# Half-steps of a decoder trunk: evictions scheduled ahead of weights' parts, three leads, a later combine, six last outputs of chunk 1

## The chip, the core and the metric

One NeuronCore of one Trainium2 chip runs the whole program; the other cores are idle. The metric is the device time of one execution in microseconds (us), lower is better. The kernel before takes 2192.76 us, the median of three runs (2188.43 to 2197.22).

## The reference

A trunk of two layers works on 512 prompt tokens and 8 sample tokens, 520 columns in all, of 1024 features. Each layer is a half-step feed-forward, a mixer (differential attention beside gated linear attention in layer 0, a matrix memory in layer 1), and another half-step feed-forward:

```python
def swiglu(x, w_gate, w_up, w_down):
    return (jax.nn.silu(x @ w_gate) * (x @ w_up)) @ w_down

def macaron_half(x, g, w_gate, w_up, w_down):
    return x + (0.5 * swiglu(rmsnorm(x, g), w_gate, w_up, w_down)).astype(x.dtype)
```

`w_gate` and `w_up` are 1024 x 2816, `w_down` is 2816 x 1024, all float32. The change touches the four half-steps and nothing else. In the order of the program the stages are: half-step 1, mixer 1, half-step 2, half-step 3, mixer 2, half-step 4. Half-steps 2 and 3 follow each other directly.

## The kernel before, in words

**Layout.** Activations lie transposed: features on 128 partitions in 8 tiles (`KT`), tokens along the columns in two chunks, chunk 0 of 256 columns and chunk 1 of 264 (`CH`). A float32 product is made of three matmuls of a narrower type: every operand is split into a rounded high part and the rest (`split`, lines 110 to 112: a cast on ScalarE, L111, then a subtraction on VectorE, L112), and `dense` (L106 to L108) issues high x high, high x low and low x high. So each weight tile costs a cast and a subtraction besides its transfer.

**A half-step** works through 22 tiles of 128 hidden features, in groups of 6, 6, 6 and 4 (`GROUPS`). The first four tiles (`LEAD = 4`) are *leads*: gate and up products in the plain way, `early`, 8 weight tiles for the gate, 8 for the up product, two chunks. While TensorE works on them, VectorE and ScalarE norm the input and form the sums and differences that the rest needs (`begin` and `then`, generators whose parts are called by `step()` between products). All later gate tiles are *units* of a seven-product scheme in the manner of Strassen and Winograd (`Unit.product`): gate and up features are one 2 x 2 side, the two halves of the features and the two chunks the other, and seven products (p1, q5, q6, p2, p3, p7, p4) of 4 weight tiles each do the work of eight. Three banks A, B and E take them: p1, q6, p7 and p4 accumulate in A one after the other, p2 in B on a copy of p1, q5 and p3 in E. So each product but the first has to wait until the one before it in its bank has been read out (evicted): `Gate.out`, with `c5` for q5 (L515), `f.h(1)` for q6 (L517), a Silu for p2 (L519), additions for p3 and p7 (L521 to L525) and a multiply for p4 (L528). p4 of a unit is issued behind p1 and q5 of the next one.

**Weights of a unit** (`weights`, L418 to L439): a transfer of g (two blocks, tag `graw`, two buffers), one of u, one of a block that is written twice into s (tag `raw`, three buffers in the pool `wraw`), all on SP's queue, and an accumulating transfer on POOL's queue (L429) that adds two further blocks into s. Then `parts` splits g, u and s, two additions (L432) turn g into further sums, and it is split again. The split halves go to the pool `whl` with five buffers. All of this is in `tc.high_priority(AHF)` with AHF = 200.

**The order of the work** is made when the kernel is built: a scheduler simulates the engines and always takes the instruction with the best priority among those that it thinks are ready; priority is the place in the program, and `tc.high_priority(n)` treats instructions as though they stood n places earlier. [...]

**Pairs.** Two gate tiles form a `Pair`, whose four results lie in one tile `h` (L452 to L456). `open` takes it: tag `stg` (one buffer) for the first pair, `graw` for the second while leads run, `stg` for the others, and a small memset on POOL. When both tiles are done, `combine` (L465 to L474) forms three sums and differences on VectorE and splits all seven parts into `hidden`, which is what the *down* units (`Down`, the second matrix, again seven products, evicted into x by L552) read. In the kernel before, both pairs of the leads are combined inside the first unit, behind its q5 (L600 to L605).

**The end of a half-step** (L636 to L651): the last group's hidden features are multiplied in the plain way, 8 outputs x 2 chunks, each 4 weight tiles x 3 matmuls. The first `KT - lag` outputs are done in both chunks; the last `lag` ones first in chunk 0 and then in chunk 1, so that the norm of chunk 0 for the next stage (`norm_lead` before another half-step, `norm_ahead` before a mixer: statistics on TensorE, a chain of short VectorE operations in `rsqrt`, then `norm_apply`, L173, with a multiply and a split per feature tile) can run beside chunk 1's outputs. `lag` is 4, and 0 in the last half-step. The split weights of these last outputs are held until chunk 1 has used them.

Of the kernel before, what the change touches and what calls it, by code (L numbers as in the profile page):

```python
# [7 lines left out]
F32 = mybir.dt.float32  # L8
# [7 lines left out]
P = 128  # L16
# [7 lines left out]
LEAD = 4  # L24
CH = ((0, 256), (256, 264))
UNIT = 8
# [11 lines left out]
AHM, AHF, AHE = 1, 200, 100  # L38
WHL = 5
# [22 lines left out]
class Net:  # L62
# [12 lines left out]
    def fetch(self, u):  # L75
        if self.raw[0] != u:
            raw = self.wraw.tile([P, UNIT * P], F32, tag="raw", name="raw")
            self.wq.dma_start(out=raw, in_=self.t["w"][u])
            self.raw = (u, raw)
# [185 lines left out]
    def half_step(self, pos, first, last, xp, hp, pa):  # L265
# [10 lines left out]
        H = KT // 2  # L276
        n0, n1 = CH[0][1], CH[1][1]
# [140 lines left out]
        def weights(f):  # L418

            B = f.nk * P  # L420
            w = self.t["w"]
            g = hp.tile([P, 4 * n1], F32, tag="graw", name="graw", bufs=2)[:, :2 * B]
            self.wq.dma_start(out=g, in_=w[f.u0, :, :2 * B])
            u = hp.tile([P, H * P], F32, tag="u2", name="u2")[:, :B]
            self.wq.dma_start(out=u, in_=w[f.u0 + 1, :, :B])
            s = self.wraw.tile([P, 2 * H * P], F32, tag="raw", name="raw")[:, :2 * B]
            s2 = s.rearrange("p (u c) -> p u c", u=2)
            self.wq.dma_start(out=s2, in_=w[f.u0 + 1, :, None, B:2 * B].to_broadcast([P, 2, B]))
            nc.gpsimd.dma_start(out=s2, in_=w[f.u0:f.u0 + 2, :, :B].rearrange("u p c -> p u c"), accum_op=ALU.add)  # L429

            def add(x, y):
                nc.vector.tensor_tensor(out=x, in0=x, in1=y, op=ALU.add)  # L432
            with tc.high_priority(AHF):
                f.w = parts(g, B, 2, ("g1", "g2"))
                f.w |= parts(u, B, 1, ("u2",))
                f.w |= parts(s, B, 2, ("s3", "s1"))
                add(g[:, :B], s[:, B:])
                add(g[:, B:], g[:, :B])
                f.w |= parts(g, B, 2, ("s2", "s4"))  # L439
# [7 lines left out]
        class Pair:  # L447

            def __init__(self, i, plain):
                self.i, self.plain, self.h = i, plain, None  # L450

            def open(self, tag="stg"):  # L452
                if self.h is None:
                    self.h = hp.tile([P, 4 * n1], F32, tag=tag, name="h",
                                     bufs=2 if tag == "graw" else None).rearrange("p (s t) -> p s t", s=4)
                    nc.gpsimd.memset(self.h[:, 0:3:2, n0:], 0.0)  # L456
# [8 lines left out]
            def combine(self):  # L465
                x11, x22, x21, x12 = [self.h[:, i] for i in range(4)]
# [8 lines left out]
        self_split = self.split  # L475
# [5 lines left out]
        class Unit:  # L481

            def product(f, kind):
# [11 lines left out]
                f.out(kind, ps[:, :n])  # L495
                step()

        class Gate(Unit):
# [11 lines left out]
            def out(f, kind, ps):  # L510
# [16 lines left out]
                elif kind == "p4":  # L527
                    nc.vector.tensor_tensor(out=f.h(0), in0=ps, in1=f.h(0), op=ALU.mult)  # L528
                    f.done(0)
                    if f.odd and not f.pair.plain:  # L530
                        f.pair.combine()
# [24 lines left out]
        for gi, nf in enumerate(GROUPS):  # L556
            plain = gi == len(GROUPS) - 1
            pairs = [Pair(i, plain) for i in range(nf // 2)]
# [12 lines left out]
        leads, seq = seq[:LEAD], seq[LEAD:]  # L571
# [7 lines left out]
        while i < LEAD:  # L579
# [4 lines left out]
            for f in fs:  # L584
                f.pair.open("stg" if i < 2 else "graw")
# [10 lines left out]
        for f in seq:  # L596
# [3 lines left out]
            if before is None:  # L600
# [3 lines left out]
                for p in (leads[0].pair, leads[2].pair):  # L604
                    p.combine()  # L605
# [6 lines left out]
            for kind in ("q6", "p2", "p3", "p7"):  # L612
                f.product(kind)
            before = f
# [22 lines left out]
        lag = 0 if last else 4  # L637
# [1296 lines left out]
```

## Time and profile before

| | us |
|---|---|
| median of three runs | 2192.76 |
| lowest, highest | 2188.43, 2197.22 |
| the profiled execution | 2194.01 |
| its span in the trace | 2192.2 |
| TensorE matmul busy | 2130.5 |
| VectorE busy | 1629.2 |
| ScalarE busy | 1108.1 |

The span runs from the first to the last instruction of the program. PE is TensorE's matmuls, PEld its weight loads, DVE VectorE, ACT ScalarE, POOL GpSimd, SP the queue that issues most transfers. A busy matmul is no sure sign of full speed, since matmuls overlap: the number started in a stretch (x415 in 50 us) says more. [...] In a row of the waits view or in brackets, "<- ACT h L655" names what ended the wait: the instruction at line 655 on ScalarE that writes tile h. Tile names are those of the program: A, B, E the banks of the units, g and u those of the leads, y those of the last outputs, pj the mixers' first tiles, c the tile of q5.

### The profile page before, as it was taken

The page shows a single profiled execution, that of the slowest core. Times are in us where ns is not written, and L with a number is a line of the kernel's source. Part 1 is how long each engine was busy: PE and PEld are TensorE (multiplying, and loading weights), DVE is VectorE, ACT ScalarE, POOL GpSimd, SP SyncE. Part 2 cuts the span into 40 slices and gives each one's busy share as a digit, 9 for nine tenths or more (in the row PEclk, how much of TensorE's full clock was granted, in tenths as well). Part 3 has the DMA queues.
Part 4 walks back from the last instruction along what each step waited for, and adds up shares of the span by engine and source line. Part 5 has one row for each costly group of instructions (what it writes and reads, how often), then busy time and mean ns, then how long its engine had stood idle before and what let it go on. Part 6 is the DMA issues. An engine that isn't in the chain of part 4 may idle for free.

```text
span 2192.2 us, 46399 instructions
## 1 busy us (share of the span) xinstructions
PE 2130.5 (97%) x17908; PEld 2001.1 (91%) x17908; DVE 1629.2 (74%) x3409; ACT 1108.1 (51%) x2080; POOL 194.6 (9%) x276
## 2 busy tenths in 40 slices
PE   8999999999999999999999999999999999999999
PEld 8899999776776799999999999998989899999999
DVE  8888887434486587888877888877745588788884
ACT  6555555334523354556554565654555456455653
POOL 1011101000000001111100111100000000111110
PEclk9999999999999999999999999999999999999999
DMA  7487764478787745867733677653554564676872
GB/s 214 118 207 169 180 169 144 155 261 264 233 264 249 240 143 128 209 159 191 186 126 84 167 179 193 161 147 94 149 158 147 167 195 152 139 204 166 191 182 73
DMA packets 175763, 381.29 MB, mean 174 GB/s; under 512 B 16353, under 2 KB 51730, under 8 KB 175414
## 3 DMA queue, kind: packets, MB, share of 16 engines
q1 hardware_dynamic: 129600, 283.23, 39.6%
q0 software_dynamic: 40176, 82.05, 20.9%
q10 hardware_dynamic: 5766, 13.05, 1.6%
q8 instruction: 140, 2.29, 0.4%
q14 instruction: 81, 0.66, 0.1%
HBM read 361.15 MB, written 17.11 MB: 173 GB/s over the span
## 4 chain that ended last, share of the span: by engine, by line
PE 74%; DVE 13%; DMA 9%; ACT 3%; issue 2%; SPq 0%; ACTq 0%; DVEq 0%; POOLq 0%
PE A L106 9%; PE A L108 8%; PE A L107 8%; PE E L106 4%; PE E L107 4%; PE E L108 4%; DVE wlo L112 4%; PE pj L106 4%; PE pj L108 3%; PE pj L107 3%; PE y L106 2%; DMA raw<-w 2%; PE y L107 2%; PE y L108 2%; PE B L108 2%; PE B L107 2%
## 5 line engine op out<-in xcount | busy, mean ns | idle before, releaser
L112 DVE TENSOR_TENSOR wlo<-raw,whi 128x512 fp32r<-128x512 f32 (+2 forms) x344 | 311.9, 910 | 106.1 <-ACT whi L111 101.6
L111 ACT CAST whi<-raw 128x512 fp32r<-128x512 f32 (+2 forms) x344 | 273.2, 799 | 153.8 <-PE pj L107 76.6
L112 DVE TENSOR_TENSOR wlo<-graw,whi 128x1024 fp32r<-128x1024 f32 (+1 forms) x240 | 266.4, 1115 | 113.3 <-ACT whi L111 112.2
L111 ACT CAST whi<-graw 128x1024 fp32r<-128x1024 f32 (+1 forms) x240 | 231.2, 965 | 154.4 <-PE B L107 90.0
L106 PE MATMUL pj<-xh,whi 128*128 128x264 f32 (+1 forms) x896 | 258.8, 291 | 4.3 <-ACT kT L655 1.5
L106 PE MATMUL A<-xb,whi 128*128 128x264 f32 (+1 forms) x864 | 250.8, 290 | 8.2 <-DVE c L524 4.7
L108 PE MATMUL pj<-xh,wlo 128*128 128x264 f32 (+1 forms) x896 | 254.3, 285 | 1.5 <-DVE wlo L112 1.5
L107 PE MATMUL pj<-xl,whi 128*128 128x264 f32 (+1 forms) x896 | 255.0, 285 | 0.8 <-DVE xl L112 0.7
L107 PE MATMUL A<-xb,whi 128*128 128x264 f32 (+1 forms) x864 | 244.7, 283 | 0.6 <-DVE xb L112 0.6
L108 PE MATMUL A<-xb,wlo 128*128 128x264 f32 (+1 forms) x864 | 245.0, 284 | 0.0
L429 POOL DMA_DIRECT2D raw<-w x120 | 142.1, 1184 | 1141.3 <-DMA raw<-w 402.7
L106 PEld LDWEIGHTS pj<-xh,whi 128*128 128x128 f32 x896 | 169.1, 189 | 20.5 <-issue 9.5
L106 PEld LDWEIGHTS A<-xb,whi 128*128 128x128 f32 x864 | 163.4, 189 | 13.4 <-DVE c L524 5.9
L107 PEld LDWEIGHTS pj<-xl,whi 128*128 128x128 f32 x896 | 169.6, 189 | 5.1 <-DVE xl L112 2.5
L108 PEld LDWEIGHTS pj<-xh,wlo 128*128 128x128 f32 x896 | 169.6, 189 | 4.5 <-issue 2.7
L106 PE MATMUL A<-hh,whi 128*128 128x264 f32 (+1 forms) x576 | 165.5, 287 | 2.0
L106 PE MATMUL E<-xh,whi 128*128 128x264 f32 x576 | 163.6, 284 | 3.9 <-ACT c L655 3.9
L107 PEld LDWEIGHTS A<-xb,whi 128*128 128x128 f32 x864 | 163.1, 189 | 0.8 <-DVE xb L112 0.8
L107 PE MATMUL E<-xl,whi 128*128 128x264 f32 x576 | 163.4, 284 | 0.0
L108 PEld LDWEIGHTS A<-xb,wlo 128*128 128x128 f32 x864 | 163.3, 189 | 0.0
L108 PE MATMUL E<-xh,wlo 128*128 128x264 f32 x576 | 163.2, 283 | 0.0
L107 PE MATMUL A<-hl,whi 128*128 128x264 f32 (+1 forms) x576 | 162.7, 282 | 0.0
(491 smaller groups left out, 6266.9 us busy)
## 6 DMA issues: line engine op xcount, KB each, us to landing
raw<-w SPq DMA_DIRECT2D x168, 512.0 KB, 4.2
raw<-w POOLq DMA_DIRECT2D x112, 512.0 KB, 6.9
graw<-w SPq DMA_DIRECT2D x72, 512.0 KB, 4.2
kt<-ckt SPq DMA_DIRECT2D x128, 256.0 KB, 4.4
vtile<-cv SPq DMA_DIRECT2D x128, 256.0 KB, 4.0
u<-w SPq DMA_DIRECT2D x72, 256.0 KB, 3.7
raw<-w SPq DMA_DIRECT2D x48, 384.0 KB, 3.7
raw<-w POOLq DMA_DIRECT2D x48, 384.0 KB, 5.6
```

The costliest lines, as they stand in the source:

```text
L106: nc.tensor.matmul(ps, lhsT=wh, rhs=xh, start=(ends[0] and i == ks[0]), stop=False, skip_group_check=open_)
L107: nc.tensor.matmul(ps, lhsT=wh, rhs=xl, start=False, stop=False, skip_group_check=open_)
L108: nc.tensor.matmul(ps, lhsT=wl, rhs=xh, start=False, stop=(ends[1] and i == ks[-1]), skip_group_check=open_)
L111: self.nc.scalar.copy(out=hi, in_=src)
L112: self.nc.vector.tensor_tensor(out=lo, in0=src, in1=hi, op=ALU.subtract)
L429: nc.gpsimd.dma_start(out=s2, in_=w[f.u0:f.u0 + 2, :, :B].rearrange("u p c -> p u c"), accum_op=ALU.add)
```

## The change

Five things, all in the half-steps. (1) The number of leads is 4 in the program's first half-step and 3 in the others; the tile that was a lead becomes a unit. (2) `f.out`, the eviction of a product, runs at `high_priority(AHO)` with AHO = 300, ahead of the weights' parts at 200; what followed p4 there, the combine, moves into a new `after` behind it. (3) `combine` runs at `high_priority(AHC)`, AHC = 100; the leads' first pair is combined behind all products of the first unit instead of inside it, the second pair inside it only where there are four leads (with three it is half a lead and half a unit, and is combined as every other). (4) The tiles of pairs: with four leads the first group's pairs take `stg`, `graw` and `raw`, with three `stg`, `raw`, `stg`; all others `stg`. For that, `raw` tiles grow from 1024 to 1056 columns. (5) `lag` is 6 instead of 4, still 0 in the last half-step.

```diff
@@ -21,7 +21,8 @@
 T = SEQ + NS
 DFF = 2816
 GROUPS = (6, 6, 6, 4)
-LEAD = 4
+LEAD = 4, 3
+
 CH = ((0, 256), (256, 264))
 UNIT = 8
 EPS = 1e-6
@@ -36,6 +37,7 @@
 REST = 4
 
 AHM, AHF, AHE = 1, 200, 100
+AHO, AHC = 300, 100
 WHL = 5
 SLOPE = [2.0 ** (-2 * (h + 1)) for h in range(4)]
 
@@ -74,7 +76,7 @@
 
     def fetch(self, u):
         if self.raw[0] != u:
-            raw = self.wraw.tile([P, UNIT * P], F32, tag="raw", name="raw")
+            raw = self.wraw.tile([P, 4 * CH[1][1]], F32, tag="raw", name="raw")[:, :UNIT * P]
             self.wq.dma_start(out=raw, in_=self.t["w"][u])
             self.raw = (u, raw)
 
@@ -274,6 +276,7 @@
 
         nc, tc = self.nc, self.tc
         H = KT // 2
+        lead = LEAD[not first]
         n0, n1 = CH[0][1], CH[1][1]
         xh, xl, x = self.xh, self.xl, self.x
         xb = [xp.tile([P, 3, H, n1], F32R, tag=f"xb{i}", name="xb") for i in range(2)]
@@ -423,7 +426,7 @@
             self.wq.dma_start(out=g, in_=w[f.u0, :, :2 * B])
             u = hp.tile([P, H * P], F32, tag="u2", name="u2")[:, :B]
             self.wq.dma_start(out=u, in_=w[f.u0 + 1, :, :B])
-            s = self.wraw.tile([P, 2 * H * P], F32, tag="raw", name="raw")[:, :2 * B]
+            s = self.wraw.tile([P, 4 * n1], F32, tag="raw", name="raw")[:, :2 * B]
             s2 = s.rearrange("p (u c) -> p u c", u=2)
             self.wq.dma_start(out=s2, in_=w[f.u0 + 1, :, None, B:2 * B].to_broadcast([P, 2, B]))
             nc.gpsimd.dma_start(out=s2, in_=w[f.u0:f.u0 + 2, :, :B].rearrange("u p c -> p u c"), accum_op=ALU.add)
@@ -446,13 +449,14 @@
 
         class Pair:
 
-            def __init__(self, i, plain):
-                self.i, self.plain, self.h = i, plain, None
-
-            def open(self, tag="stg"):
+            def __init__(self, i, plain, tag):
+                self.i, self.plain, self.h, self.tag = i, plain, None, tag
+
+            def open(self):
                 if self.h is None:
-                    self.h = hp.tile([P, 4 * n1], F32, tag=tag, name="h",
-                                     bufs=2 if tag == "graw" else None).rearrange("p (s t) -> p s t", s=4)
+                    pool = self_wraw if self.tag == "raw" else hp
+                    self.h = pool.tile([P, 4 * n1], F32, tag=self.tag, name="h",
+                                       bufs=2 if self.tag == "graw" else None).rearrange("p (s t) -> p s t", s=4)
                     nc.gpsimd.memset(self.h[:, 0:3:2, n0:], 0.0)
 
             def slot(self, odd, c):
@@ -463,6 +467,10 @@
                 self_split(hidden[0][:, self.i, j:j + b - a], hidden[1][:, self.i, j:j + b - a], self.h[:, a:b])
 
             def combine(self):
+                with tc.high_priority(AHC):
+                    self.combined()
+
+            def combined(self):
                 x11, x22, x21, x12 = [self.h[:, i] for i in range(4)]
                 cm = hp.tile([P, 4 * n1], F32, tag="cmb", name="cmb").rearrange("p (s t) -> p s t", s=4)
                 nc.vector.tensor_tensor(out=cm[:, 0:2], in0=self.h[:, 0:2], op=ALU.subtract,
@@ -472,7 +480,7 @@
                 nc.vector.scalar_tensor_tensor(cm[:, 3], cm[:, 2], -1.0, x21, ALU.mult, ALU.subtract)
                 for a in (0, 2):
                     self_split(hidden[0][:, self.i, 3 + a:5 + a], hidden[1][:, self.i, 3 + a:5 + a], cm[:, a:a + 2])
-        self_split = self.split
+        self_split, self_wraw = self.split, self.wraw
         hidden = []
         WHERE = {"p1": ("g1", "x11"), "p2": ("g2", "x21"), "q5": ("s1", "a"), "q6": ("s2", "b"), "p7": ("s3", "c"),
                  "p3": ("s4", "x22"), "p4": ("u2", "d")}
@@ -492,8 +500,13 @@
                            open_=True)
                 if kind == "p1":
                     self.evict(f.B[:, :n0], ps[:, :n0])
-                f.out(kind, ps[:, :n])
+                with tc.high_priority(AHO):
+                    f.out(kind, ps[:, :n])
+                f.after(kind)
                 step()
+
+            def after(f, kind):
+                pass
 
         class Gate(Unit):
             nk = H
@@ -527,8 +540,10 @@
                 elif kind == "p4":
                     nc.vector.tensor_tensor(out=f.h(0), in0=ps, in1=f.h(0), op=ALU.mult)
                     f.done(0)
-                    if f.odd and not f.pair.plain:
-                        f.pair.combine()
+
+            def after(f, kind):
+                if kind == "p4" and f.odd and not f.pair.plain:
+                    f.pair.combine()
 
             def done(f, c):
                 if f.pair.plain and not f.late:
@@ -555,7 +570,8 @@
         seq, gates = [], []
         for gi, nf in enumerate(GROUPS):
             plain = gi == len(GROUPS) - 1
-            pairs = [Pair(i, plain) for i in range(nf // 2)]
+            tags = ["stg"] * 3 if gi else ["stg", "graw", "raw"] if lead == 4 else ["stg", "raw", "stg"]
+            pairs = [Pair(i, plain, tags[i]) for i in range(nf // 2)]
             fs = [Gate(u0 + 2 * j, pairs[j // 2], j % 2) for j in range(nf)]
             gates += fs
             u0 += 2 * nf
@@ -568,7 +584,7 @@
             if not plain:
                 downs = [Down(u0 + 2 * d, d, nf // 2) for d in range(H)]
                 u0 += 2 * H
-        leads, seq = seq[:LEAD], seq[LEAD:]
+        leads, seq = seq[:lead], seq[lead:]
         self.seek(pos)
         if first:
             self.fetch(pos // UNIT)
@@ -576,13 +592,13 @@
             raw(0, range(KT))
         steps.append(begin())
         i = 0
-        while i < LEAD:
+        while i < lead:
             fs = leads[i:i + (2 if i == 0 else 1)]
             ws = [self.weights(2 * KT) for _ in fs]
             if first and i == 0:
                 self.x_load(KT, 2 * KT)
             for f in fs:
-                f.pair.open("stg" if i < 2 else "graw")
+                f.pair.open()
             if i == 0 and not first:
                 step()
             for c in range(2):
@@ -601,8 +617,8 @@
                 while steps:
                     step()
                 hidden += [hp.tile([P, max(GROUPS) // 2, 7, n1], F32R, tag=n, name=n) for n in ("hh", "hl")]
-                for p in (leads[0].pair, leads[2].pair):
-                    p.combine()
+                if lead == 4:
+                    leads[2].pair.combine()
             else:
                 before.product("p4")
                 if isinstance(before, Down) and before is downs[-1]:
@@ -611,6 +627,8 @@
                     p.parts(3, 4, 3)
             for kind in ("q6", "p2", "p3", "p7"):
                 f.product(kind)
+            if before is None:
+                leads[0].pair.combine()
             before = f
         before.product("p4")
         nf = GROUPS[-1]
@@ -634,7 +652,7 @@
             else:
                 self.sq_add(c, d)
         self.gi = self.nxt
-        lag = 0 if last else 4
+        lag = 0 if last else 6
         for d in range(KT - lag):
             w = self.weights(nf)
             down(d, 0, w)
```

## Rows read from the trace of the kernel before

**Rows 1.** The page, part 1: busy time, share of the span, instructions of each engine.

```profile
PE 2130.5 (97%) x17908; PEld 2001.1 (91%) x17908; DVE 1629.2 (74%) x3409; ACT 1108.1 (51%) x2080; POOL 194.6 (9%) x276
```

**Rows 2.** Windows view, full stretches: stretch, us, engines' busy (count), PEclk, DMA, GB/s.

```profile
950.00:1000.00 50.00, 49.98 (x415) 49.67 (x414) 41.41 (x72) 25.88 (x40) 6.05 (x6) 1.00 0.71 181
813.00:842.00 29.00, 29.00 (x243) 29.00 (x243) 17.85 (x23) 12.65 (x19) 4.76 (x4) 1.00 0.68 148
```

**Rows 3.** Timeline, first half-step: start, us, engine, line, names [idle before <- releaser].

```profile
72.86 1.04 ACT L111 CAST whi<-graw 128x1024 fp32r<-128x1024 f32 x1 [2.42 <-DMA graw<-w]
...
75.63 0.11 POOL L456 MEMSET h<- 128x16 f32 x1 [9.15 <-DVE cmb L472]
...
76.52 0.59 PE L106 MATMUL A<-xb,whi 128*128 128x264 f32 x1 [3.55 <-ACT h L655]
```

**Rows 4.** Windows view, first half-step, behind that wait.

```profile
76.40:79.80 3.40, 3.28 (x15) 3.28 (x16) 3.40 (x6) 1.35 (x5) 0.00 (x0) 0.50 0.12 36
```

**Rows 5.** Windows view, first units behind the leads, second to fourth half-step.

```profile
855.00:869.00 14.00, 11.73 (x94) 11.24 (x93) 10.43 (x16) 7.14 (x13) 1.17 (x1) 1.00 0.45 125
1214.00:1228.00 14.00, 11.50 (x92) 11.02 (x92) 10.39 (x16) 7.11 (x13) 1.18 (x1) 1.00 0.45 122
1898.00:1912.00 14.00, 11.87 (x96) 11.39 (x95) 10.18 (x16) 6.90 (x13) 1.17 (x1) 1.00 0.41 138
```

**Rows 6.** Timeline of ScalarE, third half-step, same place.

```profile
1215.62 1.05 ACT L111 CAST whi<-graw 128x1024 fp32r<-128x1024 f32 x1 [3.14 <-DMA graw<-w]
...
1218.04 0.38 ACT L655 ACTIVATE c<-E 128x264 f32<-128x264 f32 x1
```

**Rows 7.** Timeline of SP's queue, third half-step.

```profile
1210.47 0.90 SPq L423 DMA_DIRECT2D graw<-w  x2
```

**Rows 8.** Windows view, second into third half-step.

```profile
1144.00:1148.80 4.80, 2.17 (x17) 1.78 (x15) 4.41 (x10) 2.47 (x6) 0.00 (x0) 0.93 0.33 109
1148.80:1158.40 9.60, 9.53 (x44) 9.54 (x45) 7.88 (x27) 2.81 (x8) 0.00 (x0) 0.50 0.17 55
1158.40:1168.00 9.60, 9.60 (x79) 9.32 (x78) 6.13 (x20) 3.46 (x9) 0.00 (x0) 1.00 0.01 2
```

**Rows 9.** Waits (us, times, longest) of 1138 to 1160, then VectorE's timeline there.

```profile
PE g L106 <- ACT xh L111: 2.6, 1, 2.6
...
1146.75 1.23 DVE L112 TENSOR_TENSOR wlo<-raw,whi 128x1024 fp32r<-128x1024 f32 x1
```

**Rows 10.** Windows view, into the first and the second mixer.

```profile
368.00:379.00 11.00, 9.86 (x65) 7.64 (x64) 9.40 (x38) 5.41 (x14) 0.85 (x2) 1.00 0.77 245
1505.00:1516.80 11.80, 8.62 (x50) 7.51 (x49) 11.30 (x36) 6.64 (x17) 0.60 (x2) 0.86 0.23 64
```

**Rows 11.** Groups by shape, VectorE, 869 to 1130: count | busy, mean ns | idle.

```profile
L112 DVE TENSOR_TENSOR wlo<-graw,whi 128x1024 fp32r<-128x1024 f32 x30 | 36.5, 1224 | 18.1 <-ACT whi L111 17.9
...
L432 DVE TENSOR_TENSOR graw<-graw,raw 128x512 f32<-128x512 f32 x15 | 10.3, 684 | 0.0
...
L521 DVE TENSOR_TENSOR h<-E,h 128x264 f32<-128x264 f32 x16 | 6.8, 426 | 0.0
```

**Rows 12.** Windows view, last lead (second half-step); ahead of and within it (last).

```profile
824.00:842.00 18.00, 18.00 (x152) 18.00 (x151) 8.19 (x12) 5.60 (x9) 2.35 (x2) 1.00 0.70 137
1835.00:1872.00 37.00, 35.29 (x288) 34.63 (x288) 31.00 (x60) 20.19 (x31) 3.63 (x3) 1.00 0.62 182
1872.00:1885.00 13.00, 13.00 (x110) 13.00 (x109) 7.78 (x12) 5.30 (x9) 1.17 (x1) 1.00 0.66 134
```

**Rows 13.** First lead's start, SP's queue, and line 429 (1835 to 1912), last half-step.

```profile
1835.43 0.28 PE L106 MATMUL g<-xh,whi 128*128 128x256 f32 x1
...
1860.07 17.89 SPq L428 DMA_DIRECT2D raw<-w  x4
...
L429 POOL DMA_DIRECT2D raw<-w x6: 1173/1182/1243, 1864.4 to 1909.9; - x6
...
DMA to landing us min/median/max: 5.5/7.1/9.0
```

## The prediction

> **What bounds the kernel now.** I read the page's first part, then full stretches, then every place where TensorE starts fewer matmuls than in a full stretch, and last what ended the idle time there. TensorE is busy 2130.5 of 2192.2 us, VectorE 1629.2, ScalarE 1108.1 [rows 1]. In the long middle of a half-step TensorE starts 415 matmuls in 50 us, one per 120.5 ns, and among the leads 243 in 29 us, one per 119 ns [rows 2]. There TensorE is the bound, and only fewer matmuls help. Busy time hides stalls because matmuls overlap, so I count starts against these two rates. What can be won lies in short places: the first units behind the leads of all four half-steps, and the three passages from a half-step into the next stage.
>
> The sum is made against the profiled execution, 2194.0 us (span 2192.2 and 1.8 around it); the median of the three runs, 2192.8, lies 1.2 below. A measurement of this kernel can tell about 0.5% (11 us) from no change.
>
> **1. Three leads (second, third and fourth half-step).** A lead costs 2 x 8 weight tiles x 2 chunks x 3 = 96 matmuls, the same unit as seven products 7 x 4 x 3 = 84. It is 12 matmuls fewer, 1.43 us at 119 ns, three times: **4.3 us**. No waiting is needed for that; it is sure where TensorE is the bound.
>
> **2. First half-step, behind the leads.** TensorE stops 3.5 us for the eviction of q6, which ScalarE brings at 76.5; the memset on POOL, which opens the third pair in the buffer of the first, has waited 9.15 us for that pair's combine (L472), and ScalarE itself stood 2.42 us at a cast that wants a transfer [rows 3]. [...] With its own buffer ("raw"), the third pair waits for no combine, and the first pair's combine comes later. The cast's transfer may still be late, as one graw buffer stays taken in this half-step. I take **4.5 us**, with 0 and 5.1 as ends; the value is near the upper one because 9.15 of waiting goes to the combine and 2.42 to the transfer.
>
> **3. The same place in the other three.** In 14 us there are 94, 92 and 96 starts where 116 fit: 22 + 24 + 20 = 66 x 120.5 ns = 8.0 us [rows 5]. In the third half-step's rows ScalarE waits 3.14 us in a cast for graw, then works off further casts, and only then, 2.4 us later, the eviction of q5 (c<-E) that p3 needs [rows 6]. That transfer was issued at 1210.47, when the one free graw buffer was read for the last time; the other holds a pair [rows 7]. With the pair in "raw" both graw buffers serve the weights, and evictions go ahead of casts that are ready. Late next is d's split, which p4 of the first unit wants and which can only follow the last lead. I take **6 us** (ends 0 and 8.0), nearer the upper end because the wait that comes last, 3.14 us, is for that transfer.
>
> **4. From the second to the third half-step.** TensorE makes 17 starts in the 4.8 us before 1148.8 where 40 fit: 23 x 120.5 ns = 2.8 us, ended by the cast of the normed chunk 0 (xh). [...] Six outputs of chunk 1 instead of four put 2 x 12 x 121 ns = 2.9 us of matmuls between the last output of chunk 0 and the first lead, about the whole wait; without the pause I expect most of the low clock to go too. Against it: two more outputs bring VectorE 4 x 0.43 us into the same stretch, and a third group of weights is held, so one more split of 1.23 us falls there [rows 9], and chunk 1's statistics stay as late as before while the leads reach chunk 1 sooner. Of 7.0 I take **4.5 us** (ends 0 and 7.0).
>
> **5. Into the two mixers.** 65 starts in 11 us where 91 fit: 26 x 120.5 ns = 3.1 us; 50 in 11.8 us where 98 fit: 5.8 us [rows 10] (some of them short transposes). Of each at most 2.9 us is bought by two more outputs. Chunk 1's norm is next in line: the first tiles of the mixer give it only few matmuls of cover. I take **1.5 + 2 = 3.5 us** (ends 0 and 2.9 + 4.1, the second with its low clock).
>
> **6. What three leads cost.** A lead is also cover: 11.5 us in which VectorE works 2 splits of 1.22 and 2 evictions of 0.43 [rows 11], 3.3 us, so 8.2 us of free VectorE time go. In the last lead's stretch it is idle now 18 - 8.2 = 9.8 us in the second half-step and 13 - 7.8 = 5.2 us in the last, where another 37 - 31 = 6 us lie ahead of it [rows 12]. So the room is just used up: lateness of 0 to 3 us per half-step. In return each unit's VectorE work is three splits of 1.22, one of half that size, at most 0.7, and two additions of 0.68 [rows 11], 5.7 us, and four evictions, 1.7 us, under 10.1 us of TensorE: it fits, with half a combine beside it (six operations, by their sizes about 4 us a pair) barely. I charge **3 us** in all; the far end is rival C.
>
> The second and third pair's memsets, a changed tile size (1056 for 1024 columns in raw), and the call order of combine cost nothing: POOL works 194.6 of 2192 us [rows 1] and its queue's memsets need 0.11 us [rows 3]; if a memset falls behind an accumulating transfer on that queue, the price is up to that transfer's 7.1 us [rows 13] (rival C). A unit issues three transfers on SP and one on POOL where a lead issues two on SP: per half-step one issue more on each, beside matmuls; the four s tiles of rows 13 wait for buffers and not for SP.
>
> **Sum:** 4.3 + 4.5 + 6 + 4.5 + 3.5 - 3 = 19.8 us; 2194.0 - 19.8 = 2174.2, and 1.2 lower as a median: **2173 us**, 0.9% less.
>
> **Rivals.**
> A. *Evictions stay behind casts.* ScalarE's order is laid down when the kernel is built and nothing overtakes: in rows 6 a cast stood first and waited, and an eviction whose product had ended stood behind it. A priority helps only where both were thought ready together. If the casts still come first, parts 2 and 3 bring nothing: 2173 + 10.5 = **2184**. For it: the waits end with transfers. Against it: in three of four half-steps the transfer itself starts earlier. [...] Its chance is 0.16.
>
> B. *The wait moves to chunk 1.* The passages win their 2.9 us at chunk 0 and lose it at chunk 1's norm, whose row of 8 multiplies and 8 splits comes no sooner: parts 4 and 5 are nothing, 2173 + 8 = **2181**. For it: VectorE is busy 11.3 of the 11.8 us of the third passage [rows 10]. Against it: 9.6 us of leads at full clock [rows 8] lie before chunk 1. 0.16. A and B together: 2192, 0.06.
>
> C. *Slower: the first unit's s tile is late.* From its first transfer (SP) to the accumulating one (POOL) 4.3 us, landing 7.1 us [rows 13], cast 1.05 [rows 3], split 1.22, two additions 1.37 [rows 11], cast 1.05, split 1.22: 17 us. Now the first is issued at 1860.07, 25 us behind the first lead's start (1835.43). Leads end at 3 x 11.5 = 34.4 us, q6 needs the tile at 37.3. [...] It decides once the tile is issued later than about 20 us behind the first lead. Against it: with one lead fewer the buffer comes from the split of an earlier weight tile, and only one raw buffer is taken by a pair. 0.08.
>
> **How the numbers follow.** Forecast 0.54; A 0.16, B 0.16, both 0.06, C 0.08. All upper ends with no cost are 4.3 + 5.1 + 8 + 7 + 7 = 31.4 us, a median of 2161; the low end stands a little inside it, at 2163. The high end takes in A and B: 2190. Beyond lie both together and C, 0.14, and a tail below. Faster by over 0.5% is under 2181.8: the forecast but for its tail (0.53), B rather more than half (0.09), A two fifths (0.07): 0.69. Slower by over 0.5%, above 2203.7: C where its pauses are some us longer than worked out, 0.06. Same: the rest, 0.25.
>
> **What would show it.** One: 12 matmuls fewer in each of three half-steps. Two and three: no wait of over 0.3 us for h, c<-E or c (L524) behind the leads, and graw transfers that don't follow a last split. Four: no granted 0.50 at the third half-step's start. Six: what TensorE waits for in its first two units is not wlo or whi. Wrong would be: the same waits at the same units (A), pauses at the leads' second chunk (B), a wait for raw at the first q5 or q6 (C).

## The result, and the profile after

The kernel after takes 2160.1 us, the median of four runs (2159.0 to 2161.0), against 2193.5 before: a ratio of 0.985 (95% interval 0.983 to 0.987). It is faster by 33 us where the prediction had 20, and lies 3 us below the low end of the range, 2163. The profiled execution has a span of 2157.0 us. The first part of its page:

```profile
PE 2108.0 (98%) x17872; PEld 1987.7 (92%) x17872; DVE 1636.1 (76%) x3427; ACT 1120.7 (52%) x2095; POOL 198.1 (9%) x279
```

Against [rows 1] TensorE has 36 matmuls fewer, 12 in each of three half-steps, as worked out. It is busy 22.5 us less and idle 13 us less; the 36 matmuls are only 4.3 us of that. Now the windows behind the leads of half-steps 2 and 4, and the rest of their units; first two such stretches of the kernel before (columns as in rows 2; PEclk is the granted clock of TensorE as a share of full speed), which stand beside [rows 5]:

```profile
842.00:869.00 27.00, 24.70 (x199) 24.00 (x199) 22.68 (x35) 13.82 (x25) 2.46 (x3) 1.00 0.48 114
869.00:1122.00 253.00, 252.51 (x2077) 250.40 (x2076) 210.10 (x346) 142.14 (x229) 29.44 (x33) 1.00 0.71 179
```

and of the kernel after:

```profile
817.00:844.00 27.00, 27.00 (x227) 26.98 (x226) 22.53 (x34) 16.06 (x27) 3.64 (x4) 1.00 0.67 163
844.00:1101.00 257.00, 257.00 (x2135) 256.19 (x2134) 215.59 (x355) 146.29 (x236) 30.56 (x33) 1.00 0.72 181
1846.00:1873.00 27.00, 27.00 (x227) 26.93 (x226) 22.77 (x34) 15.58 (x27) 3.63 (x4) 1.00 0.65 154
1873.00:2130.00 257.00, 257.00 (x2132) 256.00 (x2131) 214.34 (x354) 145.16 (x234) 30.56 (x33) 1.00 0.69 173
```

In the first 27 us there are 227 starts instead of 199: 28 x 120 ns = 3.4 us. That was to be expected. But the stretch behind gains as much: 2077 starts in 253 us before, 2135 in 257 after, which is 2102 in 253; 25 x 120 ns = 3.0 us. Half-step 2 was not at its bound there, although TensorE shows 252.5 of 253 us busy.

The passage into half-step 3, after, beside [rows 8] (windows first, then TensorE's waits from 1124 to 1166):

```profile
1120.00:1126.00 6.00, 5.87 (x49) 5.66 (x48) 5.63 (x14) 3.76 (x8) 0.11 (x1) 1.00 0.27 90
1138.00:1145.00 7.00, 5.33 (x29) 5.09 (x30) 5.84 (x17) 3.58 (x9) 1.18 (x1) 0.76 0.50 80
```

```profile
PE g L108 <- ACT xb L113: 1.5, 1, 1.5
PE bc L155 <- DVE rs L147: 1.0, 1, 1.0
```

The pause ahead of the first lead is gone (49 starts in 6 us). But 13 us later TensorE waits 2.5 us for chunk 1, first for its root (rs), then for its split (xb), and the granted clock is 0.50 from 1141 to 1143, with 11 starts in these 2 us (0.76 over the 7).

For the rest I compare stretches: *units* is the time from the first matmul into bank A to the first last output (y), *leads* from the first matmul into g to the first into A, both by start times in the trace, in us; for kernels with three leads 10.1 us (84 matmuls of 120 ns) are taken off the units of half-steps 2 to 4, since one unit more stands there. A *mixer* is timed from its first matmul (pj) to the first one of its own outputs, and a *passage* from a half-step's first last output to the first matmul of the next stage.

| kernel | ratio to before (interval) | units 1 | units 2 | units 3 | units 4 |
|---|---|---|---|---|---|
| before | 1 | 282.8 | 277.9 | 278.3 | 278.0 |
| after | 0.985 (0.983 to 0.987) | 275.5 | 271.7 | 272.2 | 272.1 |
| e1: after, no priority for evictions | 0.994 (0.992 to 0.996) | 282.7 | 274.6 | 275.0 | 275.0 |
| e4: after, pair in graw | 0.991 (0.989 to 0.993) | 275.8 | 277.4 | 277.5 | 274.9 |
| e9: after, combine as before | 0.987 (0.984 to 0.989) | 279.5 | 272.0 | 272.1 | 272.0 |
| e2: after, four leads, pairs in graw, raw | 0.992 (0.990 to 0.994) | 275.6 | 273.9 | 273.1 | 273.4 |
| e13: after, four leads, pairs in raw, graw | 0.996 (0.995 to 0.998) | 277.6 | 278.0 | 277.1 | 276.7 |
| e5: before, evictions ahead | 0.996 (0.995 to 0.998) | 282.0 | 276.2 | 276.2 | 277.3 |
| e7: before, three leads | 0.998 (0.996 to 0.999) | 283.0 | 278.4 | 280.1 | 282.7 |
| e8: before, pair in raw | 0.995 (0.993 to 0.997) | 282.6 | 275.6 | 275.6 | 275.6 |
| e10: after, once more | 0.983 (0.981 to 0.986) | 275.7 | 271.8 | 272.0 | 271.9 |

So the units gain 7.3 + 6.2 + 6.1 + 5.9 = 25.5 us besides the 4.3 of matmuls. The leads of half-step 2 take 38.1 us instead of 53.0, 11.5 of it the lead and 3.4 a stretch at half clock that this execution does not have (from 789 to 800 the kernel before has a granted clock of 0.69 and 49 starts, and 0.50 and 29 starts in the last 6 us of it); those of 3 and 4 take 40.2 and 38.1 instead of 52.0 and 49.8, little more than a lead less. The passages and mixers together give 1.5 us, next to nothing: 1.5 and 2.9 us less in mixer 1 and in its outputs, 2.7 less in the passage into half-step 3, 0.8 less in the one into mixer 2, but 1.4 more in the one into mixer 1 and 5.0 more in mixer 2.

### The profile page after: what moved, and what is told of

Same layout as the page of the kernel before. It is cut to its first block, busy times and chain, and to the rows that moved or that the text cites. A ratio compares the mean times of both kernels' runs of the same rounds, so it can differ in the third digit from the quotient of the medians.

```text
span 2157.0 us, 46384 instructions
## 1 busy us (share of the span) xinstructions
PE 2108.0 (98%) x17872; PEld 1987.7 (92%) x17872; DVE 1636.1 (76%) x3427; ACT 1120.7 (52%) x2095; POOL 198.1 (9%) x279
## 3 DMA queue, kind: packets, MB, share of 16 engines
q1 hardware_dynamic: 130416, 284.02, 40.2%
## 5 line engine op out<-in xcount | busy, mean ns | idle before, releaser
L114 DVE TENSOR_TENSOR wlo<-graw,whi 128x1024 fp32r<-128x1024 f32 (+1 forms) x246 | 275.0, 1118 | 122.5 <-ACT whi L113 119.5
L108 PE MATMUL A<-xb,whi 128*128 128x264 f32 (+1 forms) x900 | 260.0, 289 | 1.7 <-DVE c L537 1.5
L109 PE MATMUL A<-xb,whi 128*128 128x264 f32 (+1 forms) x900 | 254.5, 283 | 0.5 <-DVE xb L114 0.5
L110 PE MATMUL A<-xb,wlo 128*128 128x264 f32 (+1 forms) x900 | 254.3, 283 | 0.0
L108 PEld LDWEIGHTS A<-xb,whi 128*128 128x128 f32 x900 | 169.3, 188 | 6.3 <-DVE c L537 2.5
L108 PE MATMUL E<-xh,whi 128*128 128x264 f32 x600 | 170.5, 284 | 0.0
L110 PE MATMUL E<-xh,wlo 128*128 128x264 f32 x600 | 170.4, 284 | 0.0
L109 PEld LDWEIGHTS A<-xb,whi 128*128 128x128 f32 x900 | 169.4, 188 | 0.7 <-DVE xb L114 0.7
L109 PE MATMUL E<-xl,whi 128*128 128x264 f32 x600 | 169.8, 283 | 0.0
L110 PEld LDWEIGHTS A<-xb,wlo 128*128 128x128 f32 x900 | 169.3, 188 | 0.0
L108 PE MATMUL A<-hh,whi 128*128 128x256 f32 (+1 forms) x576 | 163.0, 283 | 0.0
L109 PE MATMUL A<-hl,whi 128*128 128x256 f32 (+1 forms) x576 | 162.5, 282 | 0.0
```

The lines of the kernel that those rows point to most:

```text
L108: nc.tensor.matmul(ps, lhsT=wh, rhs=xh, start=(ends[0] and i == ks[0]), stop=False, skip_group_check=open_)
L109: nc.tensor.matmul(ps, lhsT=wh, rhs=xl, start=False, stop=False, skip_group_check=open_)
L110: nc.tensor.matmul(ps, lhsT=wl, rhs=xh, start=False, stop=(ends[1] and i == ks[-1]), skip_group_check=open_)
L114: self.nc.vector.tensor_tensor(out=lo, in0=src, in1=hi, op=ALU.subtract)
```

## The experiments

First each part taken out of the kernel after.

**e1: no priority for evictions.**

```diff
-                with tc.high_priority(AHO):
-                    f.out(kind, ps[:, :n])
+                f.out(kind, ps[:, :n])
```

> The kernel after, but evictions stand at their place in the program again, not 300 places ahead; all else as after (2160 us). Theory S (the gain is spread: in every unit of all four half-steps evictions stood behind the weights' casts and splits, which cost TensorE short waits under 0.4 us; the units of the last half-step lost 7.1 us to starts over 150 ns apart before, 1.9 after): the units of the four half-steps lose 4 to 5 us each again, 2160 + 18 = 2178 us, ratio to the kernel before 0.993. Rival F (the gain lies in the first two units alone, where the pair's buffer freed the transfers of graw): the priority is worth under 3 us, 2160 to 2163, ratio 0.985 to 0.986.

Measured: 2179.7 us. Theory S holds in its total, though not in its 4 to 5 us for each half-step: 7.2 us come back in half-step 1, 2.8 to 2.9 in each other. In half-step 2 the loss lies behind the first 27 us alone:

```profile
825.70:852.70 27.00, 27.00 (x227) 26.97 (x226) 22.43 (x34) 15.98 (x27) 3.64 (x4) 1.00 0.66 158
853.00:1110.00 257.00, 256.54 (x2112) 254.10 (x2111) 213.71 (x352) 143.78 (x233) 30.53 (x33) 1.00 0.72 180
```

The first units start 227 matmuls as in the kernel after, so there the priority isn't needed; behind them it is 2112 instead of 2135, 23 x 120 ns = 2.8 us.

Half-step 1 is then as slow as before, though its third pair has its own buffer and the combine comes later. Its timeline of ScalarE shows why:

```profile
73.73 1.05 ACT L113 CAST whi<-graw 128x1024 fp32r<-128x1024 f32 x1 [4.44 <-DMA graw<-w]
74.68 0.62 ACT L113 CAST hh<-cmb 128x528 fp32r<-128x528 f32 x1
75.21 1.04 ACT L113 CAST whi<-raw 128x1024 fp32r<-128x1024 f32 x1
76.16 0.38 ACT L672 ACTIVATE h<-A 128x264 f32<-128x264 f32 x1
```

The eviction of q6 (h<-A) stands behind a cast that waits 4.44 us for its transfer, and behind two more. With the priority (kernel after, same place) an eviction (c<-E) stands ahead of the cast for graw, and no matmul waits for h:

```profile
71.89 0.39 ACT L673 ACTIVATE c<-E 128x264 f32<-128x264 f32 x1 [0.76 <-PE E L110]
74.05 1.05 ACT L113 CAST whi<-graw 128x1024 fp32r<-128x1024 f32 x1 [1.77 <-DMA graw<-w]
```

**e5: the priority alone, on the kernel before** (`f.out` at `high_priority(300)`, combine behind it at its own).

> The kernel before with the evictions alone at 300 places ahead (combine stays at its own priority, behind p4). Theory S (evictions behind casts and splits cost every half-step): the first half-step's units gain the 7.2 us that the run without the priority lost there, the other three 3 us or more each (there the transfers of graw are still late), together 16 to 20 us: 2174 to 2178 us, ratio 0.991 to 0.993. Rival K (part 2 of the prediction: the pause of the first half-step ends with the combine of the first pair, by the buffer stg): the first half-step gains under 3 us, the whole under 12: over 2181 us.

Measured: 2186.6 us, ratio 0.996. Half-step 1 gains 0.8 us and not 7: rival K holds, in place and size, and theory S falls for this half-step. The other three gain 1.7, 2.1 and 0.8 us, under the 3 of theory S, and in half-step 2 the gain lies where e1 lost its:

```profile
839.00:866.00 27.00, 24.65 (x200) 24.02 (x199) 22.12 (x35) 13.82 (x26) 2.46 (x3) 1.00 0.45 113
866.00:1115.00 249.00, 248.69 (x2059) 247.84 (x2058) 207.72 (x344) 141.65 (x227) 29.46 (x33) 1.00 0.72 181
```

The first 27 us are as before (200 starts and 199), and behind them it is 2092 starts in 253 us instead of 2077. At the place of half-step 1's pause (ScalarE's timeline, then TensorE's waits of 58 to 100):

```profile
73.02 1.05 ACT L112 CAST whi<-graw 128x1024 fp32r<-128x1024 f32 x1 [2.35 <-DMA graw<-w]
73.97 1.04 ACT L112 CAST whi<-raw 128x1024 fp32r<-128x1024 f32 x1
75.76 0.39 ACT L663 ACTIVATE h<-A 128x264 f32<-128x264 f32 x1 [0.75 <-DVE cmb L473]
```

```profile
PE A L107 <- ACT h L663: 3.0, 1, 3.0
PE A L108 <- DVE hl L113: 2.2, 1, 2.2
PE A L108 <- DVE xb L113: 0.6, 1, 0.6
```

Now the eviction is ahead in priority but ends its wait with L473, the last operation of the first pair's combine, which frees the buffer that it writes. e1 and e5 together: the pause had two causes side by side, each enough to keep it. The buffer and the later combine without the priority (e1) give 0.1 of the 7.3 us, the priority without them (e5) 0.8.

**e9: the combine alone undone** (both pairs combined inside the first unit, no priority of 100).

> The kernel after with both pairs of the leads combined at the old place inside the first unit, and combine at its old priority. Theory G (a pause needs both causes gone: an eviction must neither stand behind a waiting cast nor behind the combine's casts and subtractions): the first half-step loses 2 to 5 us again at its first unit, the other three under 2 us each: 2164 to 2168 us, ratio 0.986 to 0.988. Rival T (the tiles of the pairs and the priority are all; the combine's place is worth nothing): 2159 to 2162 us, ratio 0.985.

Measured: 2167.4 us. Half-step 1 gives back 4.0 us, the others 0.3 at most. Theory G holds.

**e4: the second pair in graw again** (of the line that sets `tags`, the end).

```diff
-["stg", "raw", "stg"]
+["stg", "graw", "stg"]
```

> The kernel after, but with three leads the second pair lies in a graw buffer again and not in a raw one. Theory S: the transfers of graw follow a last split again, the first two units of three half-steps lose 1 to 2.5 us each again: 2163 to 2168 us, ratio 0.987 to 0.989. Rival O (with evictions ahead, a late cast no longer holds them): 2160 to 2161.

Measured: 2173.7 us, more than either theory. Units 2 and 3 give back 5.7 and 5.3 us, almost all of their gain, unit 4 2.8. Waits of 820 to 860 (all engines):

```profile
ACT whi L113 <- DMA graw<-w: 6.4, 3, 3.0
ACT whi L113 <- DVE graw L435: 4.8, 2, 2.4
...
PE A L108 <- DVE c L537: 2.8, 2, 2.1
```

Three casts wait for graw, as in [rows 6], now with the evictions ahead; the weights come too late though the evictions stand ahead. The longest wait for c falls in the third unit, 27 to 37 us behind the leads; from there on e4 is as fast as the kernel after (2071 starts in 250 us, 2096 in 253):

```profile
850.00:860.00 10.00, 7.91 (x58) 7.70 (x57) 9.14 (x14) 5.25 (x10) 1.17 (x1) 0.89 0.51 131
860.00:1110.00 250.00, 250.00 (x2071) 249.26 (x2071) 208.11 (x344) 142.20 (x228) 29.52 (x33) 1.00 0.71 180
```

**e8: the pair in raw alone, on the kernel before** (four leads; half-steps 2 to 4).

> The kernel before with the second pair of half-steps 2 to 4 in a raw buffer and nothing else. Theory I: with four leads a late graw transfer is partly covered; the pauses of the first two units (8.0 us in all) go by half, the short waits of later units stay: 2188 to 2190 us, ratio 0.997 to 0.999. Rival D: the 13 us that the pair in graw cost the kernel after come off here too: 2180 us, ratio 0.994.

Measured: 2185.7 us, ratio 0.995. Each of the three gains 2.3 to 2.7 us in its units, nearly all of the 8.0 us that part 3 counted. The ratio lies nearer to rival D's 0.994, but the places are those of theory I, whose first pauses go almost whole instead of by half. In half-step 2:

```profile
838.70:865.70 27.00, 26.58 (x220) 26.16 (x220) 24.81 (x39) 15.72 (x27) 4.23 (x5) 1.00 0.72 161
866.00:1114.00 248.00, 247.51 (x2035) 245.03 (x2034) 205.06 (x337) 138.83 (x224) 28.43 (x32) 1.00 0.72 180
```

The first 27 us gain 21 starts, and behind them it is 2076 in 253 us, as before. e1, e4, e5 and e8 together: in half-steps 2 to 4 the pair in raw cures the first units, and the priority all that comes behind.

**e7: three leads alone, on the kernel before** (pair in graw, no priority).

> The kernel before with three leads alone in half-steps 2 to 4 (pair in graw, evictions as before). Theory I (interplay: with three leads the second pair must leave the graw buffers): the first units wait for graw as in the run with the pair in graw, and for evictions on top: 4.3 us of matmuls won, 5 us or more per half-step lost: 2194 to 2204 us, ratio 1.000 to 1.005. Rival D (the effects add up: three leads are worth the 4 to 9 us by which half-steps with four leads were longer): 2184 to 2189 us, ratio 0.996 to 0.998.

Measured: 2190.5 us, ratio 0.998. The size is the one that rival D gives, but the units lose 0.5, 1.8 and 4.7 us as theory I has it; the matmuls and the shorter leads (38.4 instead of 53.0 us in half-step 2, only 11.5 of it the lead) make up for that. Casts wait for graw 6.2 us here (825 to 860), as in e4.

**e2 and e13: four leads in the kernel after.** In e2 only `LEAD = 4, 4`, whereby the pairs of the first group lie in stg, graw and raw; in e13 in stg, raw and graw.

> The kernel after with four leads in all half-steps (36 more matmuls). Theory S: three leads save 12 matmuls of 119 ns in each of three half-steps and cost no wait, so 2160 + 4.3 = 2164 us, ratio 0.987. Rival L (three leads also lose cover, part 6 of the prediction): the loss of a lead is paid back, 2160 to 2161. Rival M (the third lead's absence is most of the gain): over 2170.

> The kernel after with four leads in all half-steps and the first group's pairs in stg, raw and graw (four leads before had them in stg, graw and raw). Theory I (the free graw buffer is what the units gain by, three leads bring their 12 matmuls alone): units of half-steps 2 to 4 within 0.5 us of 272.0 us (the 282.1 of the kernel after less 84 matmuls, 10.1 us), where the run with the second pair in graw had 273.4 to 273.9: 2160 + 4.3 = 2164 to 2166 us, ratio 0.986 to 0.988. Rival D (three leads themselves save waits): units at 273.4 or more as with graw, 2168 us or more.

Measured: 2176.1 and 2186.6 us. By the time e2 is rival M. Its units lose 2.2, 0.9 and 1.2 us, e13's 6.3, 4.9 and 4.6. (More is in the whole than in the half-steps: leads and units of e2 give 9.5 us, and its mixer 2 takes 292.3 instead of 285.6 us, with no edit there.) e13 was to tell the raw buffer from three leads. Theory I falls; rival D's bounds hold, but not its "as with graw": with the second pair in raw the units are worse than with it in graw. What both kernels share is that with four leads the first group needs three buffers at once, two of them taken from the weights; with three leads it is one, and so it is in e8. That this is the reason is argued and not shown. Why raw and graw in this order are worse by 4 us than in the other is open.

**e11 and e12: fewer leads still.** `LEAD = 4, 2` and `LEAD = 3, 3`.

> The kernel after with two leads in half-steps 2 to 4. Theory W (cover is no bound as long as graw is free and evictions go first): 36 more matmuls fewer, 4.3 us, 2155 us, ratio 0.983. Rival L (part 6 of the prediction, one lead later: VectorE has 37 us of work with norms and splits for the 23 us of two leads): the first unit waits 5 us or more in three half-steps and falls to half clock there, 2170 to 2185 us, ratio 0.990 or more.

> The kernel after with three leads in the first half-step too. Theory W: 1.4 us fewer, or up to 3 with graw free there: 2157 to 2159 us, ratio 0.984. Rival L: the first half-step has more to norm under its leads (its input comes in raw), its first unit waits 3 us or more: over 2162 us.

Measured: 2169.2 and 2168.7 us, both rival L in direction. In the first 60 us of half-steps 2 and 4, e11 makes 426 and 446 starts, and in half-step 2 TensorE waits for the norm of chunk 1 (waits of 778 to 862),

```profile
778.70:838.70 60.00, 55.06 (x426) 53.87 (x425) 52.24 (x92) 33.62 (x54) 6.17 (x7) 0.94 0.58 140
1816.00:1876.00 60.00, 56.88 (x446) 55.22 (x444) 53.35 (x94) 34.74 (x57) 6.17 (x7) 0.97 0.65 165
```

```profile
PE bc L155 <- DVE rs L147: 2.6, 1, 2.6
PE ss L162 <- DVE acc L131: 2.4, 1, 2.4
```

where the kernel after makes 481 in both and has one such wait (ss, 1.7 us):

```profile
778.80:838.80 60.00, 58.28 (x481) 57.60 (x480) 54.42 (x94) 35.21 (x55) 7.34 (x8) 1.00 0.56 141
1808.00:1868.00 60.00, 58.29 (x481) 57.60 (x480) 57.18 (x99) 36.81 (x57) 6.45 (x8) 1.00 0.65 169
```

VectorE is busy 54.4 and 57.2 of the 60 us with three leads. So there is little cover left to take: part 6's bound is there, one lead later than it charged for. In e12 leads and units of half-step 1 take 334.8 us together instead of 328.4.

**e3 and e6: four last outputs of chunk 1**, everywhere (e3) or only before mixer 2 (e6).

```diff
-        lag = 0 if last else 6
+        lag = 0 if last else 4
```

> The kernel after with four last outputs of chunk 1 in place of six. Theory S with rival B of the prediction (the passage into the third half-step wins its 2.9 us pause, the mixers win at chunk 0 and lose at chunk 1): the third half-step gets its pause and its stretch at half clock back, 3 to 6 us; the mixers change by under 2 us: 2163 to 2167 us, ratio 0.987 to 0.988. Rival P (all three passages win 2.9 us): 2169 us or more.

> The kernel after with six last outputs of chunk 1 before the first mixer and the third half-step, four before the second mixer. Theory B (in the second mixer the wait only moved to chunk 1: its stretch took 285 to 292 us in four runs with six, 280.6 and 280.0 in two with four): 4 to 5 us less in the second mixer, 0.8 more ahead of it: 2156 us, ratio 0.983. Rival N (the second mixer's differences come from elsewhere in its order): 2159 to 2162 us, ratio 0.985.

Measured: 2161.5 and 2162.1 us, both ratio 0.985: this part by itself can't be told from none. In e3 the old pause is back (15 starts in 5 us, ended by xh after 2.6 us) with a granted clock of 0.56 behind it:

```profile
1127.00:1132.00 5.00, 2.30 (x15) 1.91 (x14) 4.62 (x12) 2.75 (x6) 0.11 (x1) 0.85 0.10 33
1132.00:1142.00 10.00, 10.00 (x54) 10.00 (x53) 7.03 (x25) 2.40 (x6) 1.18 (x1) 0.56 0.44 88
```

Against the kernel after, its passage into half-step 3 is 2.7 us longer and the leads behind it 0.1; its mixer 1 takes 3.6 us more but comes 1.4 earlier, its mixer 2 5.5 less and comes 0.7 later. At mixer 2 the first tiles wait in both kernels for the splits of their own weights (wlo 2.3 and whi 1.3 us in the kernel after, 1470 to 1500):

```profile
PE pj L110 <- DVE wlo L114: 2.3, 1, 2.3
PE pj L108 <- ACT whi L113: 1.3, 1, 1.3
```

That was 1.5 and 1.4 in the kernel before, and so it is in e3. So a wait did take the place of the pause, but it was chunk 1 only in half-step 3. At mixer 2 these splits are 0.7 of the 5.5 us; what makes the rest is open. e6's mixer 2, 283.5 us with four outputs, does not show the 280 that theory B wanted.

**e14: second and third pair of half-step 1 exchanged.**

> The kernel after with the first half-step's second and third pair exchanged: second in raw, third in graw. Theory I: the first unit's casts no longer wait for graw (1.8 us at 74), but the third pair takes graw until the third unit: the first half-step's units, 275.5 us with 272.1 as what the others reach, gain 0.5 to 2 us; 2158 to 2160 us, ratio 0.984 to 0.985, not to be told from the kernel after by the median. Rival D: no change or a loss of up to 3 us, as graw is missing one unit later.

Measured: 2163.1 us, ratio 0.985; its units lose 2.3 us. Rival D. No kernel has a lower median than the kernel after.

**e10: the kernel after once more.**

> The kernel after itself once more, for a second profile. Theory V (the mixers' stretches and their pieces at half clock differ from one execution to the next by some us, so kernels can't be compared there by one profile): the half-steps within 0.5 us of the first profile, mixer 2 (285.6 us, 6.8 us at half clock at 1717) off by over 1.5 us. Rival N (the order of the kernel fixes it): mixer 2 within 1 us and the pieces at half clock at the same places. Median 2160 us, ratio 0.985, in either case.

Measured: 2161.8 us; its profiled execution has a span of 2162.8 us, 5.8 more than the first. The units agree within 0.2 us in all four half-steps. The difference lies elsewhere: mixer 1 with its outputs 419.4 instead of 416.8, leads 1 and 2 2.2 and 1.7 us longer. The first 15 us of half-step 2 (it begins at 778.8 and at 783.9), in the first profile:

```profile
779.00:794.00 15.00, 13.28 (x110) 12.79 (x109) 13.16 (x35) 7.89 (x15) 1.34 (x2) 1.00 0.42 140
```

and in this one:

```profile
784.00:799.00 15.00, 13.05 (x96) 12.64 (x95) 11.50 (x30) 6.72 (x11) 1.19 (x2) 0.89 0.46 142
```

The same code gets full clock once and 0.89 the other time, 110 starts or 96. Mixer 2 is 284.6 instead of 285.6, less than theory V asked for; between kernels whose mixers have no edit it goes from 279.7 (e7) to 292.3 (e2), and whether that is their order or the execution stays open.

## Why the prediction was wrong

The direction was right, the size was not: 20 us forecast, 33 measured, and a low end that was no bound; even all upper ends together, 31.4 us, fall short. Between the two profiles, 35 us apart, part 1 brought 4.3, part 2 7.3, parts 3 and 6 together 18.2 where they had 3, and passages and mixers 1.5 where parts 4 and 5 had 8. Another 3.4 is the half clock under the leads of half-step 2 (0.50 from 794 to 800 in the kernel before), which no part counted, and about half of it differs between two executions of the kernel after. So what was too small and what was too large partly cancelled.

- **Part 1** held: 36 matmuls fewer, 4.3 us.
- **Part 3 failed in its size, and with it the range.** It took 2.7 us per half-step from 14 us behind the leads [rows 5] and called the rest full speed by one 50 us window with 415 starts [rows 2]. That window was the best of its stretch, not a typical one: the 253 us behind the first 27 us had 2077 starts, 410 in 50 us. The units gained 18.2 us in half-steps 2 to 4 where part 3 (6) less part 6 (3) had 3, and where its upper end was 8. The pauses themselves were counted well: e8 brings 7.4 us by the pair's buffer alone, in the first units. What the part put at nothing was the evictions behind casts in all later units: e5 gains there by the priority alone (2092 starts in 253 us), e1 loses it again without (2079). An upper end that counts only the pauses one has looked at bounds nothing.

What TensorE's weight loads waited for in the units of half-step 4 of the kernel before (1885 to 2166; us, times, longest) had a row on this, which the prediction left aside (over the whole program it is 7.1 us in 24 waits):

```profile
PEld A L106 <- DVE c L524: 2.1, 2, 1.6
PEld A L106 <- DVE x L552: 1.8, 6, 0.4
PEld E L106 <- ACT c L655: 1.0, 1, 1.0
```

The second row is the down units' evictions (L552), six waits of 0.3 us each, all behind the 27 us. The same view of the kernel after, 1846 to 2131, has no row. Without the priority (e1, 1861 to 2146) the row is back:

```profile
PEld A L108 <- DVE x L566: 1.7, 6, 0.4
```

These waits are 1.8 of the 3.0 us; what makes up the rest this view does not show.

- **Part 6** charged 3 us for lost cover; in the units of the kernel after nothing of it is seen. That cover is a bound at all is shown by e11.
- **Part 2** forecast 4.5 us with 5.1 as its end: 3.5 us of pause, and 1.6 for the 15 starts in 3.4 us at a granted clock of 0.50 [rows 4], where 28 would fit. It was 7.3. Of this 34 starts (4.1 us) lie in the first 27 us and 3.0 us behind them, where the part again had nothing (2062 starts in 253 us before, 2087 after):

```profile
59.00:86.00 27.00, 22.89 (x176) 22.48 (x175) 23.61 (x37) 15.32 (x27) 2.46 (x3) 0.94 0.37 87
86.00:341.00 255.00, 253.35 (x2078) 250.70 (x2077) 211.15 (x350) 141.26 (x230) 29.86 (x33) 1.00 0.69 175
```

```profile
59.00:86.00 27.00, 25.86 (x210) 25.22 (x209) 25.62 (x41) 17.91 (x33) 2.46 (x3) 1.00 0.36 100
86.00:334.00 248.00, 247.04 (x2046) 245.69 (x2045) 208.25 (x346) 138.79 (x224) 30.93 (x33) 1.00 0.72 181
```

Its reason, the combine that holds the buffer, was half of the truth: e1 shows that without the priority next to none of the 7.3 comes (0.1), e5 that the priority without the buffer and the late combine brings 0.8, and e9 that both without the late combine bring 3.3. Two waits for c, 1.5 us in all, stay there in the kernel after (58 to 100).
- **Parts 4 and 5** forecast 8 us. The 7.0 that part 4 starts from are 2.8 us of pause and 4.2 of low clock, 44 starts in 9.6 us at a granted 0.50 where the next 9.6 us have 79 [rows 8]. The pause into half-step 3 went as said (2.7 us), and against e3 that gain stays. The low clock, the rest of part 4, did not go: it came back 13 us later (0.50 from 1141 to 1143), behind the wait for chunk 1, which is rival B's mechanism without its full price. Into mixer 1 six outputs gain 2.2 us against e3, and mixer 2 loses 4.8, of which only 0.7 is explained, by its weights' splits. By the whole, where e3 shows no gain, it is rival B.
- **Rival A** was right that nothing overtakes on ScalarE (in e1 an eviction stands behind a cast that waits 4.44 us, in [rows 6] behind one that waits 3.14) and wrong that the casts would still come first: the priority is applied when the list is laid down, and evictions then stand ahead. Nor did part 3 hang on it: in e1 the first units run full without it.
- **Rival C** did not come about. No matmul of half-step 2 waits for a tile of weights behind the leads. Its price, 28 us and so 2201, was an estimate that no run shows: in each of three half-steps 5 us of lateness and the 4.2 us of low clock that part 4 counts.
- The parts do not add up, which the sum took for granted. Evictions ahead, three leads and the pair in raw bring 0.4%, 0.2% and 0.5% alone on the kernel before (e5, e7, e8), 1.1% together if they added; the whole, with the combine's place and the last outputs, is 1.5%. The intervals leave little between these two, but the units of half-steps 2 to 4 are plain: alone the three bring 4.5, -7.1 and 7.4 us there, 4.8 in sum, and together 18.2. Three leads pay only with the pair out of graw. Taken out of the kernel after one at a time, evictions and raw cost 0.9% and 0.6%. Where two causes hold the same matmul, the second cure brings what both cost.

## What to carry to other kernels

Count starts over the whole of a stretch that is taken as full, not over its best window: a busy share of 99.8% hid 3 us in 253. Where a wait has several causes in parallel (a cast ahead on the engine, a buffer not yet free, a transfer late), its price belongs to none of them alone; list all that would still hold the instruction when the named one is gone, and let the low end of the range reach as far as the whole stretch has room. When buffers are lent across uses, ask which transfer waits for their return: here it was worth 0.6% to lend a pair one of the three raw buffers instead of one of the two graw buffers (e4).

## What the runs showed of the hardware

Two executions of the same kernel were granted full clock and 0.89 of it in the same 15 us of code, with 110 and 96 starts there, and their spans differ by 5.8 us, while their units agree within 0.2 us. A difference between single profiles that lies in such places is no evidence of the edit.
